# The front of a decoder layer rearranged, and the expert weights of the down projection loaded in rows of 8 KB

## The chip, the core and the metric

One core of a Trainium2 chip runs one program. The metric is the time of one execution in device microseconds, median of three runs; one more execution was profiled, and all rows below come from it. In the rows PE is TensorE (PEld its weight loads), DVE VectorE, ACT ScalarE, POOL GpSimd, SP SyncE.

## The reference, cut to what is computed

256 tokens of width 1024 in fp32, one layer:

```python
a = rms_norm(h, mix_norm_g)
z = a @ w_in                        # 1024 x 3584: q, k, v of attention; q, f, i, g of HGRN2
q = partial_rope(rms_norm(q, q_norm_g), positions) * 64 ** -0.5     # 8 heads x 64
k = partial_rope(rms_norm(k, k_norm_g), positions)
attn = dilated_attention(q, k, v)
rec = hgrn2_mixer(q_h, f_h, i_h, g_h, lower_bound, hgrn_norm_g)     # 4 heads, state 128 x 128
h = h + concat([attn, rec]) @ w_out
m = rms_norm(h, ffn_norm_g)
h = h + moe_ffn(m, ...)             # top 4 of 32 experts, 1024 -> 2 x 1024 -> 1024, clamped SwiGLU
h = h + (p @ ple_proj) * sigmoid(h @ ple_gate)
```

## The kernel before

All weights are streamed from HBM by one list, `seq`, in tiles of 1 MB: 14 of w_in, 4 of w_out, then for each expert 8 gate/up tiles ("GU", a tile holds 128 input rows of 2048 numbers, so 8 KB in each partition) and 4 down tiles ("D", two rows of 4 KB in each partition), and at the end 4 of the PLE gate. `fill` issues the next load on SyncE's queue (L172) when a slot of the pool `slots` is free and fewer than `cap` tiles are in use; `used` gives a slot back when the tile's matmuls are written. While the mixing layer holds slots for its own tensors few are left for the weights; `cap(99)` comes just ahead of the experts. After expert 22 all engines pass a branch (L947) for experts with more than 64 tokens, which is not taken here.

The front. x is loaded into `h`, its rows are squared and summed on ScalarE (L256), and the factor 1/sqrt(mean + eps) comes from `rsqrt`: an integer guess and three Newton steps, 11 small VectorE operations (L245 to L250), used for x, for the query and key norms (L608 needs it), for the HGRN output (L578 needs it) and for the router's norm. A matmul of h with diag(factor) transposes and scales in one (L325), ScalarE empties the banks times the norm's weight into `ahi` (rounded to fp32r), VectorE writes the rest into `alo` (L330, L331). Each tile of w_in and w_out is split alike: `hi` on ScalarE (L193), `lo` on POOL or VectorE by a table (L194). Then `zchunk` runs seven chunks, each with three products hi*ahi, lo*ahi, hi*alo (L371 to L382), into one of two pairs of PSUM banks (`pz`); a pair is free again once the chunk's consumer has read it. Attention and HGRN2 are written as streams of steps between the chunks; the order on each engine is fixed when the program is built, by a scheduler with a cost model. Then come `wo` (L753 to L755), the transposes of h (L796) into `hT`, the router's logits (L806), its norm (L818 to L820) and the choice of experts.

An expert e: `onehot` and `gather_rows` (L846) pick its 64 token slots, `gather_columns` transposes them into x, `gate_up` adds the bias by a matmul from `bgu` (L1009) and runs 32 matmuls (L1016), the activation follows (L1023 to L1027, one sigmoid per expert at L1024), `hidden` transposes u (L1034), `down` runs 32 matmuls (L1047) of which f = 2j + k picks the rows j * 256 + k * 128 + partition of w_down, and `scatter` adds to the tokens (L1058).

Of the kernel before, what the change touches and what calls it, by code (L numbers as in the profile page):

```python
# [110 lines left out]
def layer(ctx, tc, A, at):  # L111
# [48 lines left out]
    def fill():  # L160
        while st["raw"] < st["cap"] and st["next"] < len(seq) and S.left() > st["keep"]:
            k = seq[st["next"]]
            st["next"] += 1
            st["raw"] += 1
            if k[0][0] == "GU":
                shape = [128, 2048]
            elif k[0][0] == "D" or k[0] == "pj":
                shape = [128, 2, 1024]
            else:
                shape = [128, 4, 512]  # L170
            t, at_ = S.new(shape, F32, "raw", True)
            sp.dma_start(t, src[k])  # L172
            raw[k] = t, at_
# [47 lines left out]
    def const(name, t=None, p=pers, q=sp):  # L221
# [18 lines left out]
    def rsqrt(y, v, tag):  # L240

        n = v.shape[1]
        a = pers.tile([128, n], F32, name="rs_a" + tag)
        b = pers.tile([128, n], F32, name="rs_b" + tag)
        dve.tensor_scalar(a.bitcast(I32), v.bitcast(I32), 1, None, op0=OP.arith_shift_right)  # L245
        dve.tensor_scalar(b.bitcast(I32), a.bitcast(I32), -1.0, float(0x5F3759DF), op0=OP.mult, op1=OP.add)
# [5 lines left out]
    def row_rstd(tag):  # L252
        ss = pers.tile([128, 2], F32, name="ss" + tag)
# [4 lines left out]
        vv = pers.tile([128, 2], F32, name="vv" + tag)  # L258
        dve.tensor_scalar(vv, ss, 1.0 / D, EPS, op0=OP.mult, op1=OP.add)
        r = pers.tile([128, 2], F32, name="rstd" + tag)  # L260
        rsqrt(r, vv, tag)
        return r
# [7 lines left out]
    def bank():  # L270
        return ps.tile([128, 512], F32, name="bk", bufs=4)
# [5 lines left out]

    rstd = row_rstd("x")
    ahi = S.new([128, 8, T], F32R, "ahi")
# [28 lines left out]
    pool.dma_start(rb, A["router_b"][0:1, :].to_broadcast([128, E]))  # L308
    tri = const("tri", q=pool, p=mp)
    slot = const("slot", q=pool)  # L310
    sel2 = const("sel", q=pool)

    p0 = bank()
    pe.transpose(p0[:, :24], rows, ident[:24, :24])
    act.activation(gcol, p0[:, :24], AF.Copy)


    dg = carve(256).rearrange("p (a d) -> p a d", a=2)
    for tt in range(2):
        dve.tensor_scalar(dg[:, tt, :], ident, rstd[:, tt:tt + 1], None, op0=OP.mult)  # L320
    for j in range(0, 8, 2):
        b = bank()
        for jj in range(2):
            for tt in range(2):
                pe.matmul(b[:, jj * 256 + tt * 128:jj * 256 + tt * 128 + 128], h[:, tt, (j + jj) * 128:(j + jj) * 128 + 128],  # L325
                          dg[:, tt, :], start=True, stop=True)
        for jj in range(2):
            s = b[:, jj * 256:jj * 256 + 256]
            g = gcol[:, j + jj:j + jj + 1]
            act.activation(ahi[:, j + jj, :], s, AF.Copy, scale=g)  # L330
            dve.scalar_tensor_tensor(alo[:, j + jj, :], s, g, ahi[:, j + jj, :].bitcast(F32), op0=OP.mult, op1=OP.subtract)  # L331

# [213 lines left out]
    def hgrn_out():  # L546
# [48 lines left out]
    def qk_norm(p, gi, dst, scale):  # L595
# [409 lines left out]
    def gate_up(e, between):  # L1005
        G, U = mm(), mm()
        x = R[e]["x"]
        for k, P in enumerate((G, U)):
            pe.matmul(P, R[e]["sel"], bgu[:, k * 512:k * 512 + 512], start=True, stop=False,  # L1009
                      skip_group_check=True)  # L1010
        for j in range(8):
            w, _ = need(("GU", e), j)
            for k, P in enumerate((G, U)):
                for n in range(2):
                    c = k * D + n * 512
                    pe.matmul(P[halves[n], :], x[:, j % 4, j // 4, :], w[:, c:c + 512], start=False, stop=j == 7, skip_group_check=True)  # L1016
# [176 lines left out]
```

## Time and profile before

| | |
|---|---|
| median of 3 runs | 1169.43 us (1166.47 to 1170.24) |
| the profiled execution | 1167.22 us, its span 1165.4 us |
| PE busy | 1080.2 us (93%) |
| DVE, ACT, POOL busy | 294.1, 201.9, 74.8 us |
| bytes moved | 432.43 MB, 371 GB/s over the span |

The span runs from the first to the last instruction. A row of a timeline gives start, duration, engine, line, operation, output<-inputs, shape and count, and in brackets how long the engine was idle before it and what ended that. Matmuls are pipelined, so a row's duration can reach past the next start.

### The profile page before, as it was taken

The numbers are of one execution on the slowest core, as the hardware profiler recorded it, in microseconds if no ns is written. First come the engines' busy times: TensorE is split into PE (matmuls) and PEld (weight loads), VectorE is DVE, ScalarE is ACT, GpSimd is POOL, SyncE is SP. The second block draws the span as 40 slices with busy tenths as digits, with TensorE's granted clock in tenths as the row PEclk, the third lists the DMA queues.
The fourth block names the chain that finished last, engine by engine and source line by source line (L and its number), as shares of the span: only waits on it lengthen the run. The fifth ranks groups of instructions, "written<-read, shape, count | busy, mean of one in ns | idle before, by whom it ended". The sixth has DMA issues, their size and how long they took to land. (4 is left out here: it accounts for less than half of the span.)

```text
span 1165.4 us, 12337 instructions
## 1 busy us (share of the span) xinstructions
PE 1080.2 (93%) x5001; PEld 451.9 (39%) x5001; DVE 294.1 (25%) x613; ACT 201.9 (17%) x366; POOL 74.8 (6%) x77
## 2 busy tenths in 40 slices
PE   5889988999999999999999999989999999999887
PEld 4778764333333333333333332223333332223226
DVE  4877744211111111111111111101111111110025
ACT  5646531000011011000000000001000000000013
POOL 4433321000000000000000000000000000000000
PEclk9989997999999999999999999999999999999999
DMA  9913568999999999999999999999998999999991
GB/s 313 338 60 103 207 227 324 415 416 417 417 416 417 417 418 418 417 417 418 417 417 417 417 417 417 405 417 417 416 415 327 418 417 417 417 418 417 418 400 46
DMA packets 87118, 432.43 MB, mean 371 GB/s; under 512 B 7736, under 2 KB 9184, under 8 KB 54288
## 3 DMA queue, kind: packets, MB, share of 16 engines
q1 hardware_dynamic: 86480, 430.35, 91.6%
q0 software_dynamic: 576, 1.23, 0.4%
q8 instruction: 41, 0.67, 0.2%
q14 instruction: 21, 0.17, 0.0%
HBM read 430.51 MB, written 1.05 MB: 370 GB/s over the span
## 5 line engine op out<-in xcount | busy, mean ns | idle before, releaser
L1016 PE MATMUL bk<-raw,x 128*64 128x512 f32 x2048 | 473.5, 596 | 12.5 <-DMA raw<-in_expert_w_gate_up 12.3
L1016 PEld LDWEIGHTS bk<-raw,x 128*64 128x64 f32 x2048 | 143.0, 137 | 311.6 <-issue 261.9
L1047 PE MATMUL bk<-raw,ht 128*64 128x512 f32 x1024 | 247.2, 598 | 12.5 <-DMA raw<-in_expert_w_down 12.5
L1047 PEld LDWEIGHTS bk<-raw,ht 128*64 128x64 f32 x1024 | 71.4, 136 | 150.9 <-issue 115.0
L1023 DVE TENSOR_SCALAR gm<-bk 128x512 f32<-128x512 f32 x32 | 22.1, 692 | 364.7 <-PE bk L1016 364.7
L1024 ACT ACTIVATE sgm<-gm 128x512 f32<-128x512 f32 x32 | 20.2, 630 | 422.5 <-DVE gm L1023 422.5
L846 PE MATMUL bk<-h,sx 128*64 128x512 f32 x256 | 66.1, 614 | 9.5 <-ACT st L1002 9.5
L997 DVE TENSOR_SCALAR sg<-c_slot,posx,gates 128x128 f32<-128x128 f32 x64 | 19.3, 344 | 213.1 <-PE bk L1000 213.1
L1058 PE MATMUL pz<-y,st 64*128 64x512 f32 x256 | 66.0, 627 | 4.0 <-ACT y L1051 2.2
L838 POOL CAST sb<-c_sel 128x128 fp32r<-128x128 f32 x32 | 9.3, 293 | 847.9 <-PE bk L1009 832.0
L194 POOL TENSOR_TENSOR lo<-raw,hi 128x1024 fp32r<-128x1024 f32 x20 | 50.1, 2526 | 84.7 <-ACT hi L193 84.7
L859 DVE TENSOR_TENSOR x<-bk,gcol 128x256 f32<-128x256 f32 x64 | 24.2, 420 | 108.8 <-PE bk L855 108.8
L1051 ACT ACTIVATE y<-bk 128x512 f32<-128x512 f32 x32 | 19.1, 597 | 145.5 <-PE bk L1047 145.5
L193 ACT ACTIVATE hi<-raw 128x1024 fp32r<-128x1024 f32 x36 | 37.8, 1056 | 22.9 <-issue 9.7
L1058 PEld LDWEIGHTS pz<-y,st 64*128 64x128 f32 x256 | 22.6, 188 | 45.7 <-issue 40.9
L380 PE MATMUL pz<-hi,ahi 128*128 128x512 f32 x80 | 33.6, 420 | 7.0 <-DVE N L608 6.8
L835 DVE TENSOR_SCALAR sx<-c_slot,posx,rstd 128x64 f32<-128x64 f32 x64 | 17.2, 312 | 79.0 <-PE bk L846 78.9
L848 ACT ACTIVATE xr<-bk 128x512 f32<-128x512 f32 x32 | 19.1, 597 | 93.7 <-PE bk L846 93.7
L382 PE MATMUL pz<-hi,alo 128*128 128x512 f32 x80 | 33.2, 415 | 0.0
L381 PE MATMUL pz<-lo,ahi 128*128 128x512 f32 x80 | 33.0, 412 | 0.0
L846 PEld LDWEIGHTS bk<-h,sx 128*64 128x64 f32 x256 | 17.4, 139 | 38.6 <-issue 24.4
L1002 ACT ACTIVATE st<-bk 128x256 f32<-128x256 f32 x32 | 12.3, 384 | 113.5 <-PE bk L1000 113.5
(266 smaller groups left out, 849.6 us busy)
## 6 DMA issues: line engine op xcount, KB each, us to landing
raw<-in_expert_w_gate_up SPq DMA_DIRECT2D x256, 1024.0 KB, 19.9
raw<-in_expert_w_down SPq DMA_DIRECT2D x128, 1024.0 KB, 20.0
raw<-in_w_in SPq DMA_DIRECT2D x14, 1024.0 KB, 13.6
raw<-in_w_out SPq DMA_DIRECT2D x4, 1024.0 KB, 5.1
raw<-in_ple_gate SPq DMA_DIRECT2D x4, 1024.0 KB, 18.9
h<-in_x SPq DMA_DIRECT2D x2, 512.0 KB, 4.2
ct<-in_consts SPq DMA_DIRECT2D x2, 512.0 KB
raw<-in_ple_proj SPq DMA_DIRECT2D x1, 1024.0 KB, 20.2
```

What stands on the lines that cost most here:

```text
L193: act.activation(hi, w[:, o:o + 2], AF.Copy)
L194: (pool if i in POOL_FIRST else dve).tensor_tensor(lo, w[:, o:o + 2], hi.bitcast(F32), OP.subtract)
L380: pe.matmul(o, ahi[:, j, s], hi[:, jj, :], start=j == 0, stop=False)
L381: pe.matmul(o, ahi[:, j, s], lo[:, jj, :], start=False, stop=False)
L382: pe.matmul(o, alo[:, j, s], hi[:, jj, :], start=False, stop=j == 7)
L846: pe.matmul(b[halves[n], :], s[:, tt, :], h[:, tt, n * 512:n * 512 + 512], start=tt == 0, stop=tt == 1, skip_group_check=True)
L859: dve.tensor_tensor(x[:, :, n, :], b.rearrange("p (c n s) -> p c n s", c=4, n=2)[:, :, n, :], g, OP.mult)
L1016: pe.matmul(P[halves[n], :], x[:, j % 4, j // 4, :], w[:, c:c + 512], start=False, stop=j == 7, skip_group_check=True)
L1023: dve.tensor_scalar(gm, G, 7.0, None, op0=OP.min)
L1024: act.activation(sg, gm, AF.Sigmoid, scale=1.702)
L1047: pe.matmul(P[halves[n], :], t[:, f % 4, f // 4, :], w[:, k, n * 512:n * 512 + 512], start=f == 0, stop=f == 7, skip_group_check=True)
L1058: pe.matmul(acc[tt][n], t[halves[n], tt * 128:tt * 128 + 128], y[halves[n], :], start=e == 0, stop=False, skip_group_check=True)
```

## The change

Five things are edited.

1. Front. The identity is loaded first. x is transposed as it is (16 transposes with the identity into four banks); the squares' sum is shared between ScalarE and VectorE; diag(factor) times a matrix of ones gives the factor as a row in all partitions (`rB`), and VectorE multiplies bank, norm weight and `rB` into a temporary, from which `ahi` and `alo` are made, 512 columns at a time. Nine matmuls of ones stand ahead of the transposes and six behind the row of factors (`busy`).
2. `rsqrt` is one power (v ** -0.5) on POOL, in all five places.
3. Loads. The small constants of POOL's queue move to SyncE's, behind the first seven loads of weights; the first tile of w_in is loaded in two halves. The subtraction for `bgu` moves from POOL to VectorE.
4. A down tile is read as `(j p k)` where it was `(j k p)`: a partition holds two neighbouring rows of w_down, 8 KB in one piece. `hidden` transposes every second column of u to match.
5. For expert 0 the two bias matmuls come behind the 32 others.

```diff
@@ add, expert, fill
-    w_dn = A["expert_w_down"][0].rearrange("e (j k p) n -> e j p k n", p=128, k=2)
+    w_dn = A["expert_w_down"][0].rearrange("e (j p k) n -> e j p k n", p=128, k=2)
...
-            sp.dma_start(t, src[k])
+            if place[k]:
+                sp.dma_start(t, src[k])
+            else:
+                for o in (0, 2):
+                    sp.dma_start(t[:, o:o + 2], src[k][:, o:o + 2])
@@ rsqrt, row_rstd
+    ident = const("ident")
     for tt in range(2):
         sp.dma_start(h[:, tt, :], A["x"][0, tt * 128:(tt + 1) * 128, :])
-    ident = const("ident")
...
-    def rsqrt(y, v, tag):
...
-        for k in range(3):
-            dve.scalar_tensor_tensor(a, v, -0.5, b, op0=OP.mult, op1=OP.mult)
-            dve.tensor_tensor(a, a, b, OP.mult)
-            dve.scalar_tensor_tensor(y if k == 2 else b, a, 1.5, b, op0=OP.add, op1=OP.mult)
+    def rsqrt(y, v):
+        pool.tensor_tensor(y, v, power[:, :v.shape[1]], OP.pow)
...
-        for tt in range(2):
-            act.activation(junk[:, tt, :], h[:, tt, :], AF.Square, accum_out=ss[:, tt:tt + 1])
+        act.activation(junk[:, 0, :], h[:, 0, :], AF.Square, accum_out=ss[:, 0, 0:1])
+        act.activation(junk[:, 1, 0:512], h[:, 1, 0:512], AF.Square, accum_out=ss[:, 0, 1:2])
+        dve.scalar_tensor_tensor(junk[:, 1, 512:], h[:, 1, 512:], 1.0, h[:, 1, 512:], op0=OP.mult, op1=OP.mult, accum_out=ss[:, 1, 1:2])
@@ the front
+    def busy(t, n, i=None):
...
+                i = pe.matmul(t[:, 0:128], ones, ones, start=True, stop=True).ins
...
+    busy(w, WARM)
+    xb = [bank() for _ in range(4)]
+    for tt in range(2):
+        for j in range(8):
+            o = j % 2 * 256 + tt * 128
+            pe.transpose(xb[j // 2][:, o:o + 128], h[:, tt, j * 128:j * 128 + 128], ident)
...
-    pool.dma_start(rw, A["router_w"][0].rearrange("(j p) e -> p j e", p=128))
+    sp.dma_start(rw, A["router_w"][0].rearrange("(j p) e -> p j e", p=128))
...
+    rr = w[:, 512:768]
+    for tt in range(2):
+        last = pe.matmul(rr[:, tt * 128:tt * 128 + 128], ones, dg[:, tt, :], start=True, stop=True)
...
+    busy(w, 6, last.ins)
+    rB = S.new([128, 2048], F32, "rB")
+    act.activation(rB[:, 0:256], rr, AF.Copy)
     for j in range(0, 8, 2):
...
+            dve.scalar_tensor_tensor(t[:, jj * 256:jj * 256 + 256], xb[j // 2][:, jj * 256:jj * 256 + 256], gcol[:, j + jj:j + jj + 1], rB[:, 0:256],
+                                     op0=OP.mult, op1=OP.mult)
+        o = ahi[:, j:j + 2, :].rearrange("p j t -> p (j t)")
+        act.activation(o, t, AF.Copy)
+        dve.tensor_tensor(alo[:, j:j + 2, :].rearrange("p j t -> p (j t)"), t, o.bitcast(F32), OP.subtract)
@@ bgu
-        pool.tensor_tensor(bgu[r, :], braw[r, :], bgu[r, :].bitcast(F32), OP.subtract)
+        dve.tensor_tensor(bgu[r, :], braw[r, :], bgu[r, :].bitcast(F32), OP.subtract)
@@ hidden
-            pe.transpose(b[:, c * 128:c * 128 + 128], u[:, c * 128:c * 128 + 128], ident)
+            o = c // 2 * 256 + c % 2
+            pe.transpose(b[:, c * 128:c * 128 + 128], u[:, o:o + 255:2], ident)
```

The order on the engines, at three places. First TensorE from its start to the first chunk, before and after (`mt` is diag(factor), `pz<-ones` the filler, `rows` the norm weights):

```order
L314 MATMUL bk<-c_ident,rows 128x24
L325 MATMUL bk<-mt,h 128x128 x16
L380 MATMUL pz<-hi,ahi 128x512
L381 MATMUL pz<-lo,ahi 128x512
L382 MATMUL pz<-hi,alo 128x512
```

```order
L289 MATMUL pz<-ones 128x128 x9
L296 MATMUL bk<-c_ident,h 128x128 x16
L338 MATMUL pz<-mt,ones 128x128 x2
L340 MATMUL pz<-c_ident,rows 128x24
L289 MATMUL pz<-ones 128x128 x6
L402 MATMUL pz<-hi,ahi 128x512
L403 MATMUL pz<-lo,ahi 128x512
L404 MATMUL pz<-hi,alo 128x512
```

The 16 matmuls that waited for the factor are now transposes that need x alone; what waits for the factor is two matmuls. Second ScalarE from the squares to the first halves of the normed x, before and after:

```order
L256 ACTIVATE junk,ssx<-h 128x1024 x2
L315 ACTIVATE gcol<-bk 128x24
L425 ACTIVATE lbe<-lbe 128x8
L193 ACTIVATE hi<-raw 128x1024 x3
L330 ACTIVATE ahi<-bk,gcol 128x256
```

```order
L257 ACTIVATE junk,ssx<-h 128x1024
L258 ACTIVATE junk,ssx<-h 128x512
L198 ACTIVATE hi<-raw 128x1024 x2
L341 ACTIVATE gcol<-pz 128x24
L344 ACTIVATE rB<-pz 128x256
L447 ACTIVATE lbe<-lbe 128x8
L198 ACTIVATE hi<-raw 128x1024
L351 ACTIVATE ahi<-rB 128x512
```

In both the first `ahi` stands behind the third `hi`. Third POOL from its first tensor operation to the experts, before and after (`rstdx`, `r_365`, `r_600`, `or_1214`, `rstd_1423` are the five factors: of x, keys, queries, HGRN output, router):

```order
L741 TENSOR_TENSOR rw<-rw,gcol 128x256
L194 TENSOR_TENSOR lo<-raw,hi 128x1024 x9
L463 MEMSET Adg 128x1024
L194 TENSOR_TENSOR lo<-raw,hi 128x1024 x9
L780 DMA braw<-in_expert_b_gate_up 32x512 x8
L194 TENSOR_TENSOR lo<-raw,hi 128x1024 x2
L838 CAST sb<-c_sel 128x128 x2
L910 TENSOR_TENSOR bgu<-braw,bgu 32x1024 x2
```

```order
L251 TENSOR_TENSOR rstdx<-vvx,power 128x2
L199 TENSOR_TENSOR lo<-raw,hi 128x1024 x6
L761 TENSOR_TENSOR rw<-rw,gcol 128x256
L251 TENSOR_TENSOR r_365<-v_363,power 128x16
L199 TENSOR_TENSOR lo<-raw,hi 128x1024 x3
L485 MEMSET Adg 128x1024
L199 TENSOR_TENSOR lo<-raw,hi 128x1024
L251 TENSOR_TENSOR r_600<-v_598,power 128x16
L199 TENSOR_TENSOR lo<-raw,hi 128x1024 x8
L800 DMA braw<-in_expert_b_gate_up 32x512 x8
L251 TENSOR_TENSOR or_1214<-ov_1213,power 128x8
L199 TENSOR_TENSOR lo<-raw,hi 128x1024 x2
```

The powers stand in POOL's line behind its subtractions: the first behind none, the second behind six, the third behind one after the memset, the fourth behind none after the loads of `braw`.

## Rows read from the trace of the kernel before

**Rows 1.** Page: span; PE busy tenths and GB/s, 40 slices:
```profile
span 1165.4 us, 12337 instructions
...
PE   5889988999999999999999999989999999999887
...
GB/s 313 338 60 103 207 227 324 415 416 417 417 416 417 417 418 418 417 417 418 417 417 417 417 417 417 405 417 417 416 415 327 418 417 417 417 418 417 418 400 46
```

**Rows 2.** The chain that ended last: start us, us, what:
```profile
1118.60 15.93 DMA raw<-in_ple_gate
```

**Rows 3.** Timeline of ACT, the sigmoid of experts 9, 17, 20, 25 and 31:
```profile
452.50 0.63 ACT L1024 ACTIVATE sgm<-gm 128x512 f32<-128x512 f32 x1 [15.13 <-DVE gm L1023]
...
677.44 0.63 ACT L1024 ACTIVATE sgm<-gm 128x512 f32<-128x512 f32 x1 [15.13 <-DVE gm L1023]
...
769.29 0.63 ACT L1024 ACTIVATE sgm<-gm 128x512 f32<-128x512 f32 x1 [18.61 <-DVE gm L1023]
...
928.45 0.63 ACT L1024 ACTIVATE sgm<-gm 128x512 f32<-128x512 f32 x1 [6.95 <-DVE gm L1023]
...
1108.90 0.63 ACT L1024 ACTIVATE sgm<-gm 128x512 f32<-128x512 f32 x1 [19.21 <-DVE gm L1023]
```

**Rows 4.** Stretches: busy us PE, PEld, DVE, ACT, POOL; PEclk, DMA share, GB/s:
```profile
460.00:470.00 10.00, 10.00 (x48) 3.37 (x46) 1.30 (x4) 1.19 (x2) 0.00 (x0) 1.00 1.03 409
470.00:490.00 20.00, 18.83 (x90) 6.32 (x86) 3.91 (x8) 2.21 (x4) 0.29 (x1) 1.00 1.02 422
```

**Rows 5.** Groups by line: busy us, mean ns, idle before, its releaser:
```profile
L1034 PEld LDWEIGHTS bk<-c_ident,um 128*128 128x128 f32 x128 | 13.4, 141 | 36.7 <-issue 18.7 <-PE bk L1047 18.0
...
L194 POOL TENSOR_TENSOR lo<-raw,hi 128x1024 fp32r<-128x1024 f32 x20 | 50.1, 2526 | 84.7 <-ACT hi L193 84.7
...
L741 POOL TENSOR_TENSOR rw<-rw,gcol 128x256 f32<-128x256 f32 x1 | 0.6, 609 | 3.9 <-ACT gcol L315 3.9
```

**Rows 6.** Timelines of PE and ACT at the start:
```profile
11.30 6.38 PE L325 MATMUL bk<-mt,h 128*128 128x128 f32 x32 [2.97 <-DVE mt L320]
17.43 0.48 PE L380 MATMUL pz<-hi,ahi 128*128 128x512 f32 x1
...
15.41 1.06 ACT L193 ACTIVATE hi<-raw 128x1024 fp32r<-128x1024 f32 x1 [0.70 <-DMA raw<-in_w_in]
```

**Rows 7.** Stretches near the start, columns as in rows 4:
```profile
5.00:10.00 5.00, 0.27 (x1) 0.18 (x1) 1.88 (x13) 2.20 (x6) 0.61 (x1) 1.00 0.87 242
10.00:15.00 5.00, 3.70 (x17) 3.71 (x18) 2.54 (x12) 2.00 (x2) 0.00 (x0) 1.00 1.05 385
...
17.40:25.50 8.10, 6.46 (x32) 4.70 (x31) 6.90 (x9) 5.59 (x11) 3.92 (x2) 1.00 1.05 390
```

**Rows 8.** Waits of PE (17 to 80 us: total, times, longest); DVE's timeline:
```profile
PE pz L380 <- DVE N L608: 6.8, 2, 3.6
...
41.48 2.37 DVE L248 SCALAR_TENSOR_TENSOR rs_aq<-v,rs_bq 128x16 f32<-128x16 f32 x1
```

**Rows 9.** Stretches, columns as in rows 4:
```profile
70.00:80.00 10.00, 7.09 (x20) 5.63 (x21) 9.61 (x27) 2.40 (x4) 0.00 (x0) 0.66 0.33 107
160.00:165.00 5.00, 5.00 (x17) 3.91 (x16) 0.82 (x2) 0.02 (x1) 0.00 (x0) 0.66 0.89 334
```

**Rows 10.** Timelines of DVE and PE at the HGRN output:
```profile
150.08 0.17 DVE L566 TENSOR_SCALAR ov<-os 128x8 f32<-128x8 f32 x1 [1.51 <-ACT mt L563]
...
156.84 2.16 DVE L578 SCALAR_TENSOR_TENSOR G<-bk,or,G 128x128 f32<-128x128 f32 x8
...
157.34 0.30 PE L584 MATMUL bk<-c_ident,G 128*128 128x128 f32 x1 [1.92 <-DVE G L578]
```

**Rows 11.** Timelines of DVE and PE at the router, and a DVE subtraction:
```profile
75.69 1.22 DVE L194 TENSOR_TENSOR lo<-raw,hi 128x1024 fp32r<-128x1024 f32 x1
...
176.47 2.19 DVE L245 TENSOR_SCALAR rs_am<-vv 128x2 int32<-128x2 int32 x1
...
179.51 3.62 PE L806 MATMUL bk<-rw,hT 128*128 128x32 f32 x16 [2.03 <-DVE hT L801]
```

More of the change, by code (lines that the diff above doesn't have):

```diff
@@ L2 @@
 from collections import deque
-from contextlib import ExitStack
+from contextlib import ExitStack, nullcontext
 import numpy as np
@@ L34 @@
 E_PLE, E_SPILL = 20, 22
+WARM = 9
 def constants():
@@ L235, in layer, with row_rstd @@
     gcol = pers.tile([128, 24], F32, name="gcol")
+    ones = pers.tile([128, 128], F32, name="ones")
+    dve.memset(ones, 1.0)
+    power = pers.tile([128, 16], F32, name="power")
+    pool.memset(power, -0.5)
     def lnexp():
         act.preload_act_table_set("natural_log_exp_and_others")
[L240 to L253 removed]
+    def rsqrt(y, v):
+        pool.tensor_tensor(y, v, power[:, :v.shape[1]], OP.pow)
+    def row_rstd():
+        ss = pers.tile([128, 2, 2], F32, name="ssx")
+        dve.memset(ss, 0.0)
         junk = S.new([128, 2, D], F32, "junk")
[L255 to L256 removed]
+        act.activation(junk[:, 0, :], h[:, 0, :], AF.Square, accum_out=ss[:, 0, 0:1])
+        act.activation(junk[:, 1, 0:512], h[:, 1, 0:512], AF.Square, accum_out=ss[:, 0, 1:2])
+        dve.scalar_tensor_tensor(junk[:, 1, 512:], h[:, 1, 512:], 1.0, h[:, 1, 512:], op0=OP.mult, op1=OP.mult, accum_out=ss[:, 1, 1:2])
         S.free()
[L258 to L261, printed above, removed]
+        vv = pers.tile([128, 2], F32, name="vvx")
+        dve.tensor_tensor(vv, ss[:, 0, :], ss[:, 1, :], OP.add)
+        dve.tensor_scalar(vv, vv, 1.0 / D, EPS, op0=OP.mult, op1=OP.add)
+        r = pers.tile([128, 2], F32, name="rstdx")
+        rsqrt(r, vv)
         return r
@@ L276, in pz @@
         return ps.tile([128, 1024], F32, name="pz", bufs=2)
-    rstd = row_rstd("x")
+    w = pz()
+    def busy(t, n, i=None):
+        for k in range(n):
+            with tc.issue_after(i) if i is not None else nullcontext():
+                i = pe.matmul(t[:, 0:128], ones, ones, start=True, stop=True).ins
[5 more added lines that the diff above has]
+            pe.transpose(xb[j // 2][:, o:o + 128], h[:, tt, j * 128:j * 128 + 128], ident)
+    rstd = row_rstd()
     ahi = S.new([128, 8, T], F32R, "ahi")
@@ L305, in layer @@
     rw = mp.tile([128, 8, E], F32, name="rw")
-    pool.dma_start(rw, A["router_w"][0].rearrange("(j p) e -> p j e", p=128))
+    sp.dma_start(rw, A["router_w"][0].rearrange("(j p) e -> p j e", p=128))
     rb = mp.tile([128, E], F32, name="rb")
[L308 to L315, printed above, removed]
+    sp.dma_start(rb, A["router_b"][0:1, :].to_broadcast([128, E]))
+    tri = const("tri", p=mp)
+    slot = const("slot")
+    sel2 = const("sel")
     dg = carve(256).rearrange("p (a d) -> p a d", a=2)
@@ L320, in layer @@
         dve.tensor_scalar(dg[:, tt, :], ident, rstd[:, tt:tt + 1], None, op0=OP.mult)
+    rr = w[:, 512:768]
+    for tt in range(2):
+        last = pe.matmul(rr[:, tt * 128:tt * 128 + 128], ones, dg[:, tt, :], start=True, stop=True)
+    p0 = w[:, 768:792]
+    pe.transpose(p0, rows, ident[:24, :24])
+    act.activation(gcol, p0, AF.Copy)
+    busy(w, 6, last.ins)
+    rB = S.new([128, 2048], F32, "rB")
+    act.activation(rB[:, 0:256], rr, AF.Copy)
     for j in range(0, 8, 2):
-        b = bank()
+        t = rB[:, 512 + 512 * (j // 2 % 2):1024 + 512 * (j // 2 % 2)]
         for jj in range(2):
[L324 to L331, printed above, removed]
+            dve.scalar_tensor_tensor(t[:, jj * 256:jj * 256 + 256], xb[j // 2][:, jj * 256:jj * 256 + 256], gcol[:, j + jj:j + jj + 1], rB[:, 0:256],
[3 more added lines that the diff above has]
+        dve.tensor_tensor(alo[:, j:j + 2, :].rearrange("p j t -> p (j t)"), t, o.bitcast(F32), OP.subtract)
+    S.free()
     streams = [deque(), deque()]
@@ L737, in layer @@
     drain(1)
-    ones = mp.tile([128, 128], F32, name="ones")
-    pool.memset(ones, 1.0)
     pool.tensor_tensor(rw, rw, gcol[:, 8:16, None].to_broadcast([128, 8, E]), OP.mult)
@@ L1007, in gate_up, with bias @@
         x = R[e]["x"]
-        for k, P in enumerate((G, U)):
-            pe.matmul(P, R[e]["sel"], bgu[:, k * 512:k * 512 + 512], start=True, stop=False,
-                      skip_group_check=True)
+        def bias():
+            for k, P in enumerate((G, U)):
+                pe.matmul(P, R[e]["sel"], bgu[:, k * 512:k * 512 + 512], start=e > 0, stop=e == 0, skip_group_check=True)
+        if e:
+            bias()
         for j in range(8):
@@ L1015, in gate_up @@
                     c = k * D + n * 512
-                    pe.matmul(P[halves[n], :], x[:, j % 4, j // 4, :], w[:, c:c + 512], start=False, stop=j == 7, skip_group_check=True)
+                    pe.matmul(P[halves[n], :], x[:, j % 4, j // 4, :], w[:, c:c + 512], start=e == 0 and j == 0, stop=j == 7 and e > 0,
+                              skip_group_check=True)
             used(("GU", e), j, 0)
@@ L1019, in gate_up @@
                 f()
+        if not e:
+            bias()
         gm = wp.tile([128, 512], F32, name="gm")
```

6 lines of the change are left out of this document (3 added, 3 removed).

## The prediction

> **What bounds the kernel now.** I read the page first, then the chain of waits, then stretches of the timeline. The reader is to see three parts. (1) From the eighth of the 40 slices (204 us) on the bytes moved stand at 415 to 418 GB/s, but for one of 405, one of 327 (the branch on the overflow) and the last two [rows 1]. So from about 200 us on the stream of expert weights is never idle, save at the branch. (2) The chain that ended last is made of transfers there, the last of them the gate's, with the tail of TensorE work behind it [rows 2]. (3) Before 200 us the bytes fall as low as 60 GB/s: there the weights wait for slots that the mixing layer frees, and TensorE sets the pace. The time is therefore: front, plus bytes over rate, plus tail. A microsecond taken from the front moves the whole stream forward, and so does a faster stream; the tail is not edited.
>
> TensorE is a close second in the stream. By the sigmoid that each expert does once, eight experts from 452.50 to 677.44 take 28.1 us each: there TensorE eats tiles that were loaded ahead and goes at its own pace. From 928.45 to 1108.90 six take 30.1 each, from 677.44 to 769.29 three take 30.6 [rows 3]: there it waits for data. Its margin is 6 x 2.0 + 3 x 2.5 = 19.5 us.
>
> **8 KB rows.** The queue is 8 gate/up tiles, then 4 down tiles, for each expert. In one period the rate is 409 GB/s for ten microseconds and 422 for twenty [rows 4], which is the share of the down tiles (two rows of 4 KB a partition) and of the gate/up tiles (one of 8 KB). A tile of 1.049 MB costs 2.564 us at 409 and 2.485 at 422, 0.079 less; 32 x 4 = 128 tiles, **10.1 us**. Bounds: 0, if it isn't the row that makes the difference, and 10.1; I take 10.1, since everything but the row is alike in the two kinds. TensorE can follow: 19.5 us of margin are more than 10.1. The price is hidden()'s transpose, which now loads every second column of u. Rows show 141 ns for each such load of neighbouring columns [rows 5] and none with a stride; bounds 0 and twice as long, 4 x 0.14 = 0.56 us an expert. I take 0: it is off the path as long as TensorE waits.
> The Trainium skill, "DMA: Bandwidth & Descriptors", section Specifications, puts full rate at 512 B and above; by it the 4 KB rows would already run at full rate and this term would be 0. The trace differs (409 against 422).
>
> **The front.** Here I sum what TensorE loses before 193 us and what of it the edits take away.
>
> Start. The first matmul of the first chunk stands at 17.43 [rows 6]. After the change the raw transposes need x and the identity only, and the factor comes as a row. What then ends last is in ScalarE's order: the first ahi stands behind the third hi, which needs the second weight tile. That hi ran at 15.41, when its tile landed [rows 6]. Five small loads of POOL's queue (304 KB in short rows) are now behind seven weight loads on SyncE; the slice in which they ran moved 242 GB/s, the next 385 [rows 7]. At 385 that slice would carry (385 - 242) x 5 = 0.7 MB more, 1.9 us. So hi at 13.5, 1.06 for it, 0.6 for an ahi of 512 columns (as the sigmoids of [rows 3]): first matmul at 15.1, **2.3 us**. From there to 25.5 us TensorE was busy for 6.5 of 8.1 us [rows 7], for want of ahi, alo and a lo; now a pair of ahi comes each 1.66 us (hi and ahi), so the fourth and last at 20.1. I take **1.0**. The 15 filler matmuls and the 16 transposes lie before the weights are split and cost nothing unless they reach past 15 us: 31 at the 0.2 to 0.4 us that the first ones took (6.38 us for 16 matmuls in 32 records) is 6 to 12 us from about 1 us on, with the wait for x inside. Their cover is the landing of the weights.
>
> Query and key norms. TensorE waited 6.8 us in two places for N, which frees its PSUM pair: 3.6 the second time, so 3.2 the first [rows 8]. In N's chain stand 11 small VectorE operations; one of them took 2.37 us beside a POOL subtraction, where most take 0.17 [rows 8]. One power on POOL takes the place of all 11. A power on POOL is not in the trace: below, nothing; above, the 0.6 us of a product of 256 columns [rows 5], for the new ones have 2 to 16. I take 0.3. But it queues behind POOL's own subtractions of 2.5 us [rows 5]: in the order, behind six and the router product the first time, and behind one after the memset the second. What waits behind it on POOL is the next subtraction, whose weight tile TensorE needs some 5 us later. Both waits go: **3.2** and **3.6**. With the second, the granted clock need not fall: it was 0.66 from 70 to 80 us [rows 9], 6.8 us at the lower level (1.2 GHz). Of the 2.9 us that TensorE was idle in these ten I put half there, so it worked for 5.3 us at that level and lost half: **2.6**.
>
> HGRN output. The same chain began at 150.25 and ended at 156.8; TensorE then waited 1.9 us for G [rows 10]. With the power first on POOL, ahead of the two subtractions, G follows at 150.6 and takes its 2.2 us, so it is whole near 153, before TensorE's 155.4: **1.9**, and the clock's 0.66 from 160 to 165 [rows 9], 3.4 us at half speed, **1.7**.
>
> Router. TensorE waited 2.0 us for hT, which stood behind a step of 2.19 us beside POOL's bgu [rows 11]. bgu now runs on VectorE, ahead of the second hT: 2 x 1.2 us (a subtraction of 1024 columns there [rows 11]). hT ends at 177.8, not 179.45: **1.7**. The Newton steps left lie beside these matmuls. Moving the bias matmuls of expert 0 behind its others changes no sum.
>
> Together 18.0 us. All of it only if nothing else is late next. TensorE runs nearly without gaps in slices four and five (87 to 146 us) [rows 1], its order is fixed ahead, and once it is 10 us earlier VectorE and ScalarE must be so too; the order after 80 us is new. I take **14**; bounds 4 (the start and little more) and 19. The stream can follow the front: in slices three to six it moved 60 to 227 GB/s for 116 us [rows 1], so the tiles loaded ahead fit.
>
> **Sum.** 14 + 10.1 = 24.1. The profiled execution took 1167.2 us with a span of 1165.4, so 1143.1 by it; it lies 2.2 below the median of the runs, 1169.4, and against that I forecast 1145.3, rounded 1145.
>
> **Rivals.**
> A. The front's waits only move: POOL's queue holds the powers back, or VectorE's chain is late next. For it: POOL's rows of 2.5 us, ahead of two of the powers. Against it: TensorE has no other large wait for VectorE before 150 us. Front 4: 1169.4 - 14 = 1155. Chance 0.17.
> B. Rows of 4 KB already move at full rate, and the 409 has another cause (an access pattern of the down weights in HBM, which the edit leaves). Front alone: 1169.4 - 14 = 1155. For it: the same bytes lie in the same megabyte of HBM before and after. Against it: the two kinds of tile differ in the row alone [rows 4]. Chance 0.06. It is what the rule of the Trainium skill's page named above comes to.
> C. The strided weight load makes TensorE the bound. Without its waits the last sigmoid would be at 1108.9 - 19.5 - 14 = 1075; the stream puts it at 1108.9 - 24.1 = 1085. So 32 experts may grow by 0.3 us each for nothing. At twice the load time (0.56 an expert) it is 1093, and the time 1154. **Slower than before** it gets from 1.16 us an expert on (1075 + 37 = 1112 against 1109), that is 0.29 us more for each load of 141 ns. For it: no row shows a stride. Against it: the load lies beside other matmuls mostly. Chance 0.05 for the doubling, 0.04 for slower, about 1175. The Trainium skill, "SBUF — State Buffer", section Door 1, has lines of 16 bytes that want two hits each; every second fp32 gives two, so by it the stride is free. No run here shows it.
> D. All of the front's waits go, with a shorter norm at the router too: 1169.4 - 10.1 - 21 = 1138. Chance 0.10.
>
> **Numbers.** The forecast, 1139 to 1151, has 0.58. The range takes in A, B, the doubling and D: 1135 to 1157. About 0.3% (3.5 us) is what a measurement of this kernel can tell from no change. Faster 0.94, same 0.02, slower 0.04.
>
> **What would show it.** Rows: the rate in the down tiles' third of a period is 420 or more. Front: first chunk matmul near 15, no wait of TensorE for N or G, the clock full from 70 to 80, expert 0's sigmoid at about 196 where it was at 210. Stream: late experts at 29.8 us each, TensorE still waiting for data. Wrong it is if the sigmoids late in the stream show no wait for data (C), if the third stays at 409 (B), or if new waits of TensorE stand before expert 0 (A).

## The result, and the profile after

The changed kernel takes 1154.7 us (median of six runs, 1152.9 to 1158.4), the kernel before 1166.5 beside it: ratio 0.9898, 95% interval 0.988 to 0.9916, so 11.8 us faster. The forecast was 1145 (1139 to 1151 with a chance of 0.58), its range 1135 to 1157: the time lies in the range, outside the narrower bounds, and about half of the 24 us came. Medians leave out one slow execution, of the kernel without fillers: 1398 us at a mean granted clock of 0.75. The profiled execution took 1153.85 us with a span of 1152.1, 13.3 less than in [rows 1].

The page of the changed kernel: span, TensorE's busy tenths and GB/s over 40 slices.
```profile
span 1152.1 us, 12336 instructions
...
PE   7989898999999999999999999989999999999887
...
GB/s 310 364 46 114 195 314 356 359 421 418 421 418 420 420 419 421 419 420 419 419 420 419 420 419 420 410 420 419 420 416 353 421 419 421 419 420 419 419 404 44
```
From the ninth slice on the stream runs at 418 to 421 GB/s, where [rows 1] have 415 to 418, but for 410, 416, 353 (the branch) and the last two slices. The bytes moved by 250 us are 270 GB/s x 250 us against 260, 2.5 MB or 6.0 us of stream more.

Stretches of the changed kernel, columns as in [rows 4].
```profile
460.00:470.00 10.00, 10.00 (x48) 3.23 (x46) 0.00 (x0) 0.28 (x1) 0.00 (x0) 1.00 1.02 422
470.00:490.00 20.00, 18.83 (x88) 6.47 (x86) 4.66 (x10) 2.81 (x5) 0.29 (x1) 1.00 1.01 418
250.00:700.00 450.00, 435.65 (x1992) 149.45 (x1991) 75.38 (x162) 44.89 (x80) 4.70 (x16) 1.00 1.01 420
```
The last of them, of the kernel before:
```profile
250.00:700.00 450.00, 435.77 (x2000) 147.71 (x1996) 75.92 (x164) 45.46 (x81) 4.70 (x16) 1.00 1.02 417
```
The dip to 409 in [rows 4] is gone, but the mean of 420 is not the 422 of the gate/up tiles before.

Timeline of ScalarE, sigmoids of experts 0, 9, 17, 27 and 31.
```profile
203.18 0.63 ACT L1050 ACTIVATE sgm<-gm 128x512 f32<-128x512 f32 x1 [7.70 <-DVE gm L1049]
...
447.20 0.63 ACT L1050 ACTIVATE sgm<-gm 128x512 f32<-128x512 f32 x1 [15.13 <-DVE gm L1049]
...
673.29 0.63 ACT L1050 ACTIVATE sgm<-gm 128x512 f32<-128x512 f32 x1 [15.13 <-DVE gm L1049]
...
976.31 0.63 ACT L1050 ACTIVATE sgm<-gm 128x512 f32<-128x512 f32 x1 [16.74 <-DVE gm L1049]
...
1096.00 0.63 ACT L1050 ACTIVATE sgm<-gm 128x512 f32<-128x512 f32 x1 [19.28 <-DVE gm L1049]
```
The sigmoid of expert 0 in the kernel before:
```profile
210.16 0.63 ACT L1024 ACTIVATE sgm<-gm 128x512 f32<-128x512 f32 x1 [6.41 <-DVE gm L1023]
```
Expert 0 is 7.0 us earlier, not 14. From expert 0 to 31 it is 892.8 us; before it was 1108.90 (in [rows 3]) less 210.16, 898.7. So in these two executions 7.0 came from the front and 5.9 from the stream. While TensorE sets the pace an expert takes 28.26 us ((673.29 - 447.20) / 8; 28.12 by [rows 3]); the late ones take 29.92 ((1096.00 - 976.31) / 4) and wait for data as before.

TensorE's waits from 10 to 182 us: total, times, longest.
```profile
PE pz L402 <- DVE N L630: 3.4, 1, 3.4
PE pz L402 <- ACT ahi L351: 2.0, 1, 2.0
PE bk L550 <- DVE W L524: 1.9, 1, 1.9
PE pz L404 <- DVE alo L352: 1.8, 1, 1.8
...
PE bk L826 <- DVE hT L821: 1.6, 2, 1.1
...
PE bk L550 <- DVE Adg L554: 1.0, 1, 1.0
...
```
One of the two waits for N, and the wait for G, are gone ([rows 8, 10]). One wait for N is as long as before, and four stand there that TensorE did not have, or had for 0.2 us: at the start for ahi and alo, and two for VectorE at the HGRN levels (W, Adg). From 110 to 142 us TensorE's waits add up to 3.9 us; for the kernel before none is listed there.

Timelines of POOL, then VectorE, in the front.
```profile
7.91 0.71 POOL L251 TENSOR_TENSOR rstdx<-vvx,power 128x2 f32<-128x2 f32 x1 [7.05 <-DVE vvx L263]
...
36.97 2.90 POOL L251 TENSOR_TENSOR r<-v,power 128x16 f32<-128x16 f32 x1
...
64.32 2.90 POOL L251 TENSOR_TENSOR r<-v,power 128x16 f32<-128x16 f32 x1 [2.52 <-DVE v L625]
...
115.64 5.70 POOL L199 TENSOR_TENSOR lo<-raw,hi 128x1024 fp32r<-128x1024 f32 x2 [13.30 <-ACT hi L198]
...
147.59 1.66 POOL L251 TENSOR_TENSOR or<-ov,power 128x8 f32<-128x8 f32 x1 [4.09 <-DMA raw<-in_expert_w_gate_up]
...
115.69 3.40 DVE L511 TENSOR_TENSOR W<-hbf 128x1024 f32<-128x1024 f32 x1
...
121.41 1.20 DVE L511 TENSOR_TENSOR W<-hbf 128x1024 f32<-128x1024 f32 x1
```
The powers take 0.71, 2.90, 2.90 and 1.66 us: 0.155 a column and 0.42 beside it, by the two longer sorts ((2.90 - 1.66) / 8). Beside POOL's subtraction from 115.64 a VectorE step takes 3.40 us that takes 1.20 alone.

Stretches of the changed kernel in the front, columns as in [rows 4].
```profile
70.00:80.00 10.00, 10.00 (x40) 8.11 (x39) 10.00 (x18) 3.44 (x6) 2.87 (x1) 0.86 0.31 105
160.00:165.00 5.00, 5.00 (x24) 4.04 (x24) 1.29 (x2) 1.34 (x4) 0.00 (x0) 1.00 0.09 34
170.00:175.00 5.00, 3.02 (x20) 2.91 (x20) 2.32 (x20) 0.53 (x2) 0.70 (x1) 0.67 0.99 378
180.00:185.00 5.00, 3.79 (x12) 1.34 (x12) 1.29 (x4) 0.60 (x1) 0.00 (x0) 0.50 0.98 413
205.00:210.00 5.00, 4.58 (x16) 2.04 (x18) 0.27 (x1) 0.60 (x1) 0.29 (x1) 0.66 0.66 277
```
The clock is full from 160 to 165 and 0.86 from 70 to 80, 0.66 in both before ([rows 9]). But at 180 to 185, where expert 0 now begins, it is 0.50, and 0.66 again after expert 0.

### The profile page after: what moved, and what is told of

Its sections match the earlier page's. It is cut to its first block, busy times and chain, and to the rows that moved or that the text cites. A ratio compares the mean times of both kernels' runs of the same rounds, so it can differ in the third digit from the quotient of the medians.

```text
span 1152.1 us, 12336 instructions
## 1 busy us (share of the span) xinstructions
PE 1080.9 (94%) x5019; PEld 456.1 (40%) x5019; DVE 291.7 (25%) x569; ACT 200.2 (17%) x363; POOL 81.5 (7%) x75
## 5 line engine op out<-in xcount | busy, mean ns | idle before, releaser
L199 POOL TENSOR_TENSOR lo<-raw,hi 128x1024 fp32r<-128x1024 f32 x20 | 55.9, 2813 | 51.9 <-ACT hi L198 42.3
L198 ACT ACTIVATE hi<-raw 128x1024 fp32r<-128x1024 f32 x36 | 37.3, 1052 | 21.3 <-issue 10.4
L1061 PE MATMUL bk<-c_ident,um 128*128 128x128 f32 x128 | 23.6, 308 | 12.8 <-DVE um L1053 12.8
```

The source lines that it names most:

```text
L198: act.activation(hi, w[:, o:o + 2], AF.Copy)
L199: (pool if i in POOL_FIRST else dve).tensor_tensor(lo, w[:, o:o + 2], hi.bitcast(F32), OP.subtract)
L1061: pe.transpose(b[:, c * 128:c * 128 + 128], u[:, o:o + 255:2], ident)
```

## The experiments

Each is the changed kernel with one edit, but for the first and the last two; ratios are to the kernel before, run beside it on the same chip. The kernel before took 1166.5 us beside the changed kernel and 1167.0 to 1168.2 beside the three groups of experiments, so a difference in microseconds from the changed kernel is good to about 2, and the ratios say more.

**8 KB rows alone.** The kernel before, with the two pieces of the stream's edit:
```
-    w_dn = A["expert_w_down"][0].rearrange("e (j k p) n -> e j p k n", p=128, k=2)
+    w_dn = A["expert_w_down"][0].rearrange("e (j p k) n -> e j p k n", p=128, k=2)
...
+            o = c // 2 * 256 + c % 2
+            pe.transpose(b[:, c * 128:c * 128 + 128], u[:, o:o + 255:2], ident)
```


> The kernel before with the 8 KB rows of the down weights and the strided transposes alone; its front is untouched. Theory 1 (the trace after: all tiles then run at about 420 GB/s, so a late expert takes 29.92 us, not 30.1, and nothing beyond that): about 6 us faster, ratio 0.995, the down third of a period at 420. Theory 2 (the prediction's own size, the down tiles rise to 422 and the gate/up tiles keep 422): 10.1 us, ratio 0.991, late experts at 29.8 us. Rival (rows of 4 KB were at full rate): no change, the down third still at 409. In all three the strided weight loads cost nothing late in the stream; their mean is read from the groups.

Measured: 1160.1 us, ratio 0.9927 (0.9904 to 0.9951). A stretch of it:
```profile
460.00:470.00 10.00, 9.53 (x46) 3.23 (x44) 1.90 (x6) 1.58 (x3) 0.00 (x0) 1.00 1.02 423
470.00:490.00 20.00, 18.83 (x88) 6.37 (x86) 3.37 (x6) 1.61 (x3) 0.30 (x1) 1.00 1.01 420
250.00:700.00 450.00, 435.55 (x1992) 148.69 (x1990) 75.91 (x164) 45.51 (x81) 4.74 (x16) 1.00 1.01 421
```
The mean is 421 (its front, the same as before, ran 1.8 us later in this one execution). A late expert takes 29.85 us ((1102.58 - 983.20) / 4 by its sigmoids), and expert 0 to 31 takes 890.6, 8.2 us less than before. So between the two theories: 8.2 of 10.1. The mean of all tiles is 421, below the 422 that the gate/up tiles had; why they do not keep it no run shows.

**The front alone**: the changed kernel with those lines put back.

> The changed kernel with the 4 KB rows and the neighbouring columns put back; only the front and the tail's bias differ from before. Theory 1 (the front gained 5.9 us of bytes by 220 us, because TensorE's lead of 10 us at the start of expert 0 was partly lost in expert 0): 6 to 7 us faster than before, ratio 0.994. Theory 2 (the prediction's size): 14 us, ratio 0.988. Rival (the front's waits only move, no gain at the stream): within 2 us of before. The late experts go back to 30.1 us, the down third to 409 GB/s.

Measured: 1161.0 us, ratio 0.9939 (0.9916 to 0.9962); expert 0's sigmoid at 202.11, expert 1's at 224.72 (6.7 before the 231.42 of the kernel before). Theory 1. What none expected: its stream is slower than that of the kernel before with the same rows.
```profile
250.00:700.00 450.00, 434.46 (x1992) 147.68 (x1992) 75.37 (x162) 44.84 (x80) 4.69 (x16) 1.00 1.02 416
```
The kernel before has 417 in the same 450 us, and its late experts take 30.10 us, these 30.17.

**Rows of 4 KB everywhere**, the down weights as in the run before and:
```
-    w_gu = A["expert_w_gate_up"][0].rearrange("e (j p) n -> e j p n", p=128)
+    w_gu = A["expert_w_gate_up"][0].rearrange("e (j k p) (h n) -> e h j p k n", p=128, k=2, h=2)
...
```


> The changed kernel with rows of 4 KB everywhere: the down weights as before, and each gate/up tile read as two rows of 4 KB a partition from two places instead of one of 8 KB (the columns then meet the wrong rows, so that the output isn't the reference's; bytes, tiles and matmuls are the same). If the row's length sets the rate: every tile at 409 GB/s, a late expert 30.8 us, and 256 tiles x 0.079 = 20 us more than with the front alone, about 1180 us, ratio 1.012. If another thing of the down weights (their place in memory) made the 409: gate/up tiles stay at 420 to 422, late experts 30.1 us, ratio 0.994 as with the front alone.

Measured: 1178.1 us, ratio 1.0087 (1.0061 to 1.0112).
```profile
460.00:470.00 10.00, 10.00 (x46) 3.36 (x48) 0.00 (x0) 0.00 (x0) 0.00 (x0) 1.00 1.03 410
470.00:490.00 20.00, 18.84 (x90) 6.41 (x88) 4.66 (x10) 2.80 (x5) 0.29 (x1) 1.00 1.02 409
250.00:700.00 450.00, 431.14 (x1964) 145.05 (x1962) 75.37 (x162) 44.83 (x80) 4.69 (x16) 1.00 1.02 409
```
All of it runs at 409, a late expert takes 30.71 us, and the time is 17 us over the front alone, for 20 expected. The row's length sets the rate, not the place of the down weights in memory.

**The slots' place.** By the sizes of the tiles ahead of them, the new front's small tiles move the weight slots from byte 416 to byte 32 of 512 (in every partition; 19 of the 21 slots). 384 unused bytes move them back:
```
-    power = pers.tile([128, 16], F32, name="power")
+    power = pers.tile([128, 16], F32, name="power"); pers.tile([128, 96], F32, name="pad")
```


> The changed kernel with 384 unused bytes a partition ahead of the weight slots, so that the slots begin where those of the kernel before begin (at byte 416 of 512, not 32); every engine's order is the same. Both kernels with the new front stream slower than the two with the old front (419.5 against 421.0 GB/s with 8 KB rows, 415.9 against 417.0 without). Theory 1 (the slots' place in SBUF makes it: the front's new small tiles shifted them by 128 bytes): 421 GB/s, late experts 29.82 us, about 3 us faster than the changed kernel, ratio to before 0.987. Rival (something else of the front, such as the loads moved to SyncE's queue): 419.5 GB/s and 29.92 us as in the changed kernel, ratio 0.990.

Measured: 1153.2 us, ratio 0.9878 (0.9858 to 0.9898).
```profile
250.00:700.00 450.00, 435.67 (x1992) 149.50 (x1990) 75.36 (x162) 44.91 (x80) 4.74 (x16) 1.00 1.01 421
```
421 again, late experts at 29.82 ((1095.43 - 976.15) / 4). Theory 1, for the rate, and every other trace agrees: the two kernels together below, with the slots at byte 416, have late experts at 29.81, those with 8 KB rows and the slots left where the new front puts them at 29.92 to 29.95. The time of 1.5 us less is within what single runs scatter.

**Query and key factors by small steps again** (newton is the rsqrt of the kernel before; its four tiles move the slots once more, late experts stay at 29.92).
```
-        rsqrt(r16, v16)
+        newton(r16, v16, "q%d" % gi)
```


> The changed kernel with the query and key norms' factors made by VectorE's eleven small steps again; the other norms keep the power on POOL. Theory (the power of 128x16 took 2.90 us, as long as eleven steps of 0.17 us with one of them stretched): the waits for N stay as they are in the changed kernel (3.4 us in all) give or take 1.5 us, the time within 1.5 us of the changed kernel. Rival (it was the power that took the first wait away): 3 to 7 us of waits for N again, and 2 to 4 us slower than the changed kernel.

Measured: 1155.5 us, ratio 0.991 (0.9894 to 0.9925), the time of the changed kernel. The waits didn't stay as the theory had it:
```profile
PE pz L413 <- DVE N L641: 5.8, 2, 3.0
```
Both waits for N are back (3.4 once in the changed kernel), and yet nothing is lost by 140 us. To see where a lead goes I counted TensorE's work: every matmul begun by a time, from the first of the chunks to the last ahead of expert 0, each at the spacing that it has at full clock (140 us in all). The lead is that of a kernel over the kernel before, in us; the last two columns are the leads of the sigmoids.
```
at us                      30    50    70    80   110   140   165   e0    e1
changed                   0.1   4.0   1.2   5.3   7.2   1.5   7.3   7.0   5.6
small steps, q and k      1.3   0.5   0.0   2.3   3.2   1.2   7.1   8.7   7.2
small steps, G, router   -1.0   2.8   0.2   3.0   4.6  -0.6   0.9   0.6  -0.8
POOL's last twelve moved  0.3   4.3   1.4   5.3   6.0   2.8   8.0  10.1   8.7
router kept busy         -1.3   2.8   0.0   2.8   4.4  -0.8   4.8   6.9   5.5
```
Each row is one execution, and a lead differs from one to the next: the four with the changed kernel's front (changed, front alone, slots moved, bias first) have 5.9 to 8.4 at 110, 0.1 to 2.6 at 140 and 6.0 to 8.1 at 165, and the kernel of the 8 KB rows alone, with the old front, stands 2.1 to 2.4 behind the kernel before. What a stage takes or gives is steadier: from 110 to 140 the four lose 5.7 to 6.0, from 140 to 165 they gain 5.5 to 5.9.

The powers give about 4 us by 110 (7.2 against 3.2), and 5.7 are lost again by 140, where TensorE's waits, for W and Adg above all, are 3.9; with small steps only 2.0 are lost there.

**G's and the router's factors by small steps again** (the same edit for v8 and vv2, with the 384 unused bytes, so that the slots stay at byte 32).

> The changed kernel with the factors of the HGRN output's norm and of the router's norm made by VectorE's eleven small steps again; the other norms keep the power, and the weight slots stand at the same bytes. Theory (of the changed front's gain, the HGRN output carries most: counted in TensorE's work done, the lead over the kernel before went from 1.5 us at 140 us to 5.7 at 160): the wait for G of 2 us is back, with a granted clock below 1.00 after it, the lead at 165 us falls from 7.3 to 4 us, the time rises by 2 to 4 us against the changed kernel, ratio to before 0.993. Rival (the lead there comes from the order of the work, not from the power): the wait stays away, within 1 us of the changed kernel.

Measured: 1159.2 us, ratio 0.9925 (0.9908 to 0.9943), by the medians 4.5 and by the ratios 3.2 us slower than the changed kernel, with intervals that overlap.
```profile
PE bk L617 <- DVE G L611: 2.2, 2, 2.0
```
The wait is back, and from 140 to 165 us the lead grows by 1.5, where the four with the new front gain 5.5 to 5.9. The theory holds by the trace: here lies most of what the front gives.

**POOL's last twelve subtractions on VectorE.**
```
-POOL_FIRST = [1, 3, 4, 5, 8, 9, 12, 14, 16, 17, 18, 20, 23, 25, 28, 30]
+POOL_FIRST = [1, 3, 4, 5]
```


> The changed kernel with the twelve subtractions (lo) that POOL makes from 53 us on given to VectorE; POOL keeps the first eight. Theory (a VectorE step beside such a subtraction takes two to three times as long, 3.40 us instead of 1.21, so that POOL's help costs VectorE more than the 1.22 us that it would need itself, and VectorE's chain is what is late between 55 and 135 us): TensorE's waits for VectorE from 60 to 135 us (3.4 + 1.9 + 1.0 + 0.4) fall below 4 us, TensorE's lead over the kernel before at the HGRN output grows from 1.5 us to 4 or more, and the time falls by 2 to 4 us. Rival (VectorE has no room: 12 x 1.22 = 14.6 us more work in a stretch where it is busy for 80 to 100%): more waits, 2 to 5 us slower.

Measured: 1152.6 us, ratio 0.9884 (0.9866 to 0.9902), 2.1 us below the changed kernel with intervals that overlap. The steps of W, groups by line, of the changed kernel and then of this one:
```profile
L511 DVE TENSOR_TENSOR W<-hbf 128x1024 f32<-128x1024 f32 x5 | 8.2, 1646 | 0.0
L524 DVE TENSOR_TENSOR W<-W,hqk 128x512 f32<-128x512 f32 x6 | 6.3, 1045 | 0.0
```
```profile
L511 DVE TENSOR_TENSOR W<-hbf 128x1024 f32<-128x1024 f32 x5 | 6.1, 1212 | 3.4 <-PE bk L532 3.4
L524 DVE TENSOR_TENSOR W<-W,hqk 128x512 f32<-128x512 f32 x6 | 4.1, 681 | 0.0
```
The steps beside POOL are whole again, and VectorE, with 14.6 us more work, is no later by 140; but the lead at 140 is 2.8, not 4, and the wait for N is 3.3 as before. From 110 to 140 it loses 3.2, not 5.7 to 6.0. So POOL's help costs what it brings, and is a part of the loss before 140, not all. The Trainium skill, "SBUF — State Buffer", section Who interferes with whom, says that a VectorE instruction with two inputs in SBUF contends with a GpSimd instruction that reads SBUF; the mean of 1646 against 1212 ns agrees.

**Without the six fillers** behind the factor (`busy(w, 6, last.ins)` taken out).

> The changed kernel without the six filler matmuls behind the norm's factor (the nine at the start stay). In the changed kernel ScalarE's copy of the factor waited 2.93 us for them. Theory: the copy runs some 2.5 us sooner and the first chunk's first matmul at about 14, not 16.0; of these 2 us little is left at expert 1 (0 to 1 us), since VectorE's chain is late in the middle of the front. Rival: without them the granted clock stays low longer at the start (0.66 to 0.85 from 10 to 25 us with them), the first chunk takes 1 to 2 us more, and nothing or less is gained.

Measured: 1155.3 us, ratio 0.9905 (0.9887 to 0.9923): no difference. In its profiled run the factor's copy ran at 10.93, not 14.02, and the first chunk began at 14.42, not 16.02, so the copy was held by the fillers as the theory says. That execution, at the highest mean clock of the four (0.988), took 1146.9 us; the three others, at 0.980 and 0.981, took 1155. What the start gains is smaller than what the clock takes. Its expert 0 is the earliest of all traces:
```profile
195.65 0.63 ACT L1049 ACTIVATE sgm<-gm 128x512 f32<-128x512 f32 x1 [7.70 <-DVE gm L1048]
```
That is 14.5 us earlier than before, the forecast's 14 in full, in an execution whose clock was low from 11.2 to 21.4 us and then not again until 168.2. How much of it is the edit and how much the clock one execution can't tell.

**Expert 0's bias first again.**

> The changed kernel with expert 0's bias matmuls ahead of its others again, as in the kernel before. Theory (at the end of expert 0 TensorE runs the two bias matmuls, waits 2.8 us for um and is granted 0.66 of its clock from 205 to 210 us, where the kernel before kept 1.00; with the bias at the front of the expert the gap shortens and the clock stays up): TensorE regains 1 to 2 us by expert 1, the stream's dip after 205 us (277 and 261 GB/s) shrinks, and the time falls by 1 to 2 us against the changed kernel. Rival 1: the bias waits for bgu at the start of expert 0, whose matmuls start later: 0 to 2 us slower. Rival 2: the clock falls all the same, no difference.

Measured: 1152.0 us, ratio 0.9865 (0.9844 to 0.9886). Its clock after expert 0, where the changed kernel has 0.66 and 277 GB/s:
```profile
205.00:210.00 5.00, 4.23 (x22) 1.84 (x22) 0.63 (x1) 0.60 (x1) 0.29 (x1) 1.00 1.03 410
```
The wait for um is 2.4 us, not 2.8, and expert 1's sigmoid comes at 224.63, not 225.86, 1.2 us earlier, as the theory says. In the profiled run the last expert's isn't earlier (1095.93 against 1096.00), and the intervals just overlap: seen in one trace for expert 1, likely for the time.

**The router kept busy**: eleven fillers in TensorE's gaps, four behind the first transposes of logits(0), five behind logits(1), two behind the first gather.
```
+            busy(po[0], 4, i.ins)
...
+    busy(po[0], 5, last.ins)
...
+        if e == 0:
+            busy(po[0], 2, i.ins)
```


> The changed kernel with eleven more filler matmuls in TensorE's three gaps at the router (4 where it waits for hT, 5 where it waits for the choice of experts, 2 where it waits for the gathered rows). In the changed kernel the granted clock is 0.5 from 171.7 to 185.3 us, after two gaps of TensorE, and the first matmuls of expert 0 run in it (16 in 4.72 us, the next 16 in 3.65). Theory (it is the gaps that bring the low clock, and the low clock costs expert 0 about 3 us): with TensorE at work the clock stays at 1.00 there, expert 0's sigmoid comes 3 to 4 us earlier, at about 199.5, and the time falls by 2 to 4 us. Rival 1: the clock falls all the same, no gain. Rival 2: the fillers run at the low clock, 0.47 us each, and hold up the router's matmuls behind them: 1 to 3 us slower.

Measured: 1153.9 us, ratio 0.9867 (0.9846 to 0.9887). Stretches of it:
```profile
170.00:175.00 5.00, 4.51 (x41) 4.40 (x41) 2.88 (x6) 1.02 (x3) 0.70 (x1) 1.00 1.00 416
175.00:180.00 5.00, 4.68 (x22) 4.05 (x22) 4.19 (x28) 0.53 (x2) 0.00 (x0) 0.50 0.98 374
180.00:185.00 5.00, 4.43 (x20) 1.75 (x18) 1.94 (x9) 0.60 (x1) 0.00 (x0) 0.82 1.00 419
```
The clock is full from 170 to 175 (0.67 in the changed kernel), 0.50 in the next five and 0.82 after them: the low stretch is 6.8 us long, not 13.6. From 140 us to expert 0's sigmoid this kernel gains 7.7 us of lead, the changed one 5.5 (front alone 5.4, slots moved 4.0). So half of what was expected; the low clock was shortened, not removed. The time is that of the changed kernel, within the intervals.

**Together.** Bias first, slots at byte 416 and the twelve subtractions on VectorE; then the same with the router kept busy.

> The changed kernel with three of the edits tried singly: expert 0's bias matmuls first, the weight slots back at byte 416 of 512, POOL's last twelve subtractions on VectorE. If their effects add (TensorE's lead at expert 1 larger by 1.2 and by 3.1 us, the stream at 421 instead of 419.5 GB/s, which is 2.9 us): 5 to 7 us faster than the changed kernel, ratio to before 0.984 to 0.985. Rival (what the front gives is given back in expert 0 or at the branch, or lies within the scatter of the granted clock): 3 us, ratio 0.9875.

> The kernel of the run before this one, with the eleven filler matmuls in the router's gaps. If the low clock at the start of expert 0 goes with them: another 2 to 4 us, ratio to before 0.981. If not: as without them, or up to 2 us slower.

Measured: 1151.6 us, ratio 0.9859 (0.9836 to 0.9883), and 1149.7 us, ratio 0.983 (0.9806 to 0.9855). The first, by the medians 3.1 and by the ratios 4.6 us below the changed kernel, lies between its two expectations by its ratio, and its interval overlaps that of the changed kernel slightly. The second is faster than the kernel before and the changed kernel, with intervals apart; against the first it is 1.9 us less, with intervals that overlap, so what the fillers gave there isn't shown.

## Why the prediction came out half right

**8 KB rows**, 10.1 us: the mechanism held, the size not. The step that failed is "everything but the row is alike", with 422 for all tiles after. All tiles at 8 KB run at 421, which is 8.2 us; and the changed kernel, its slots at other bytes, at 419.5 to 420, which leaves 5.9. Rival B falls with the run of 4 KB rows everywhere (409). With it falls, for rows of 4 KB here, the rule of the Trainium skill, "DMA: Bandwidth & Descriptors", section Specifications, that 512 B and above move at full rate. The strided weight loads take 209 ns on average, not 141:
```profile
L1061 PEld LDWEIGHTS bk<-c_ident,um 128*128 128x128 f32 x128 | 17.8, 209 | 38.9 <-PE bk L1074 22.0 <-issue 17.0
```
4 x 0.068 = 0.27 us an expert lie beside other matmuls for the most part: an expert at TensorE's own pace takes 0.1 us longer, and the late ones wait for data anyway. Rival C's price is off the path, as the prediction took it. But the stride isn't free, though the prediction read that in the Trainium skill, "SBUF — State Buffer", section Door 1: 209 ns against 141, and the row decides.

**The front**, 14 us, gave 7.0 at expert 0. By its steps:
- Start, 2.3 and 1.0: the first chunk began at 16.02, 1.4 earlier. The forecast had not seen that the copy of the factor stands behind six fillers in one PSUM tile, at the low clock. By 30 us the lead was 0.1.
- Waits for N, 3.2, 3.6 and 2.6 of clock: the first went and the lead rose to 4.0 at 50. The second stayed, for the power of 16 columns takes 2.90 us, not 0.3, which is 2.6 of the 3.4 waited; POOL was free when it came. The bound above, 0.6, was taken from a product and was too low by five times. The low clock near 70 us lasted 3.4 us, where it was 6.8. And what the powers do give by 110 us is lost by 140: rival A, in the middle of the front. The prediction took 4 us off for what is late next; the middle alone took 5.7.
- HGRN output, 1.9 and 1.7: 5.8 measured from 140 to 165, since there the power (1.66 us) runs first on POOL, as said, and VectorE's late work is made up too. Undone, with the router's factor, that gain falls to 1.5 and the kernel is 3 to 4.5 us slower.
- Router, 1.7: the lead grew from 7.5 at the last output matmul to 10.4 at the last logit, 2.9: 1.5 by the wait for hT (2.03, now 0.49), and 1.2 since the last 16 matmuls took 2.38 us, not the 3.62 of [rows 11], which ran at the low clock.
- Expert 0: taken at nothing, it cost 3.4. From its gather to its sigmoid it took 26.05 us (177.13 to 203.18), before 22.64 (187.52 to 210.16). The low clock lasts till 185.3 by the trace, 8 us into it, where it was 3 before. Where it reached 4 us into it, without fillers and with small steps for queries and keys, it took 24.52: so about 1.5 of the 3.4 are the clock's. Most of the other 1.9 is the order's, with the bias behind all the others: with the bias first and the low clock 3 us into it, in the last kernel together, it took 22.50. Then 1.4 more were lost by expert 1, which comes 22.68 us after expert 0 (before 21.26, with the bias first 21.35). That "moving the bias matmuls of expert 0 behind its others changes no sum" was wrong: with the bias first the kernel is 2.7 us faster by the medians.

The two bias matmuls of expert 0 in the changed kernel, the last thing ahead of its sigmoid:
```profile
201.92 0.73 PE L1030 MATMUL bk<-bgu,sb 128*128 128x512 f32 x2
```

So what was to be lost to "nothing else is late next", 4 us of the sum of 18, was 11. The time is the 1155 of rivals A and B, but that is luck: A had 4 from the front and 10.1 from the rows, B 14 and nothing, and the runs show 7.0 and 5.9. Rival D, in which every wait goes, is 17 us off.

**What would show it**: down third at 420 or more: yes. First chunk near 15: 16. No wait for N or G: one for N stays. Clock full at 70 to 80: 0.86. Expert 0 at 196: 203. Late experts at 29.8: 29.92. TensorE waiting for data at the end: yes.

**Open**: which other chain than POOL's subtractions makes VectorE late between 110 and 140 us, and how far each run's clock decides. Of the six timed runs of the changed kernel the one at a mean granted clock of 0.986 took 1152.9 us, the one at 0.980 took 1158.4; their median is 0.984, that of the kernel before in its three groups 0.986 to 0.988. At 0.9 us for each 0.001 ((1158.4 - 1152.9) / 6) that is an estimate of 2 to 4 us that the new front gives back to the clock; no run holds the clock alone. The loads moved to SyncE and the first tile in two halves were not tried by themselves either.

## What to carry to other kernels

A wait that is taken away pays only as far as the next engine's lateness: follow the lead from stage to stage, not from wait to wait. An operation that no row shows is best priced by something of its own kind: a power on POOL costs 0.16 us a column and 0.4 beside it; against eleven VectorE steps it paid at the HGRN output (8 columns), and at queries and keys (16) it took one wait away without a gain in the time. A tile added ahead of others moves them; look where the buffers of a saturated stream begin.

## What the runs showed of the hardware that was not expected

- Stream rate by row and place: 8 KB rows 421 GB/s with the slots at byte 416 of 512, 419.5 to 420 at byte 32; with a third of 4 KB rows 417 and 416; with all of 4 KB 409. Why the place matters no run shows.
- TensorE's granted clock is at 1.00 or 0.50 (2.4 or 1.2 GHz), and in runs of the same front it was low at different times: in the changed kernel from 69.3 to 72.7 and 171.7 to 185.3 us, in the one with the slots moved not at all near 70, but from 10.4 to 24.1, from 126.5 to 129.9 and from 170.8 to 187.9.
- A filler matmul of 128 columns costs 0.47 us at the lower level (2.84 us for six in the changed kernel), so that work meant to hold the clock delays what stands behind it when the clock is low already.
